# Two logarithms per head take a sooner place in the scheduler's order: a hybrid GLA and gated DeltaNet layer on one core

## The chip, the core and the metric

The kernel runs on one core of a Trainium2 chip. A core has five engines that work side by side, each through its own queue of instructions in a fixed order: TensorE (PE, matrix products; PEld is its weight load), VectorE (DVE), ScalarE (ACT, functions such as Exp and Ln), GpSimd (POOL) and SyncE (SP, which issues most transfers). Semaphores tie the queues together. The metric is the time of one execution on the device in microseconds; three runs of the kernel before have the median 2810.88 us (2809.46 to 2811.22).

## The reference

One inference step of one layer, for a prompt of 512 frames and a sample of 64 frames, all in float32:

```python
log_a = jax.nn.log_sigmoid((a_lr @ gla_wg + gla_bg).astype(f32)) / GLA_GATE_NORM
o_a, s_gla = blocked_recurrence(gla_step, st_gla, (q * dk**-0.5, k, v, log_a), block)     # 4 heads
o_a = from_heads(o_a, gla_norm) * silu(a_r)
qkv = silu(causal_dwconv(concat([b_q, b_k, b_v]), st_conv, gdn_conv_w))
o_b, s_gdn = blocked_recurrence(gdn_step, st_gdn, (l2norm(q), l2norm(k), v, g, beta), block)  # 8 heads
o_b = from_heads(o_b, gdn_norm) * silu(b_g)
x = x + g1 * (concat([o_a, o_b]) @ w_out)
x = x + g2 * conv_ffn(rmsnorm(x, norm2) * (1 + sc2) + sh2, ...)
y = rmsnorm(x, final_norm)
```

Before it stand an adaLN modulation (`silu(c) @ w_ada`) and the input projection `h @ w_in`. `gla_step` sums the gate `log_a` along the frames of a block and uses the exponentials of differences of these sums as decays. The change touches `log_sigmoid` alone.

## The kernel before, in words

Every float32 product is made of three matmuls with a high and a low part (`mm6`): a weight tile is loaded (`raw`), ScalarE rounds it to the high part (`wh`), VectorE subtracts to get the low part (`wl`); `split` does this with three buffers for each part. A projection tile of 128 columns (`in_tile`, `gemm`) takes 16 k-tiles of six matmuls each, and ends in one of two PSUM tiles `g`, from which ScalarE evicts it.

The kernel goes through a head (norm, modulation, first projections), the mixing phase (all other projections of `w_in`, with the recurrences in between), the first half of `w_out`, its second half, and the FFN with a last norm. In the mixing phase `tick` is called after each k-tile. It advances the recurrences, which are Python generators: jobs (`gdn`, `gla`, one step per tick in turn) and tasks (`gdn_conv`, `gla_gate`, every one at each tick). A planner keeps a rough clock for each engine (`charge`, called by `_Timed`), and a generator goes on only when its clock says that its results are there. This planner fixes the order in which instructions are traced.

A scheduler then sets the order on each engine from what is ready, by rank. An instruction's rank is its place in the traced order. Within `tc.high_priority(offset=80)` an instruction ranks 80 places sooner. Jobs go through `self.jv` and `self.ja`, which wrap each call so (`_Sooner`, `JOB_AHEAD = 80`, L2180 in the profile); weight conversions rank 80 sooner too (`AHEAD`). Tasks use `self.tv` and `self.ta`, which are timed in the same way but keep their place (L2204). The table loads that ScalarE needs when it changes from one set of functions to another are put in after this order is set.

`gla_gate` makes the gate of one GLA head, for the prompt (128x512, tile `m`) and the sample (128x64, tile `sq`) together. With z the projected gate it computes min(z, 0) - ln(1 + exp(-|z|)): matmuls with `wg`, an addition of the bias on VectorE, then on ScalarE two Abs, two Exp and two Ln, traced in this order in one step of the generator, then on VectorE a subtraction and the running sums (`tensor_tensor_scan`). The prompt's sums are used by the head's `gla` job; the sample's are written to memory (`put_s`, `sd_ag`) and read back by the last job, `gla_samples`, which starts with head 3. The four gates are spawned by `gla_heads`, one per head, each behind the head's `aq` and `ak` tiles. Before them, for the preceding head, stand the `ar` tiles, evicted by ScalarE with Silu into `gt` (three buffers, freed when the job has multiplied by the gate) and `ts`.

In the profile the prompt's logarithm reads `m<-m,consts` and the sample's `sq<-sq,consts`, since their bias is a constant one; Abs and Exp read `m<-m` and `sq<-sq`. All calls through a wrapper carry the wrapper's line.

Of the kernel before, what the change touches and what calls it, by code (L numbers as in the profile page):

```python
# [11 lines left out]
AF = mybir.ActivationFunctionType  # L12
# [91 lines left out]
class Kern:  # L104
# [1251 lines left out]
    def gla_gate(self, h, g, done):  # L1356

        V, A, T = self.tv, self.ta, self.jt
        y, gss, ys = self.m(), self.half()[:, :TS], self.half()[:, :TS]
        one = self.c["ones"]  # L1360
        parts = ((g, y, 0, TP, P), (gss, ys, TP, TS, TS))
        pss = [self.bank() for _ in parts]
        for ps, (z, t, c0, n, seg) in zip(pss, parts):
            T.matmul(ps[:, :n], self.wg[:, h * P:(h + 1) * P], self.na[:, c0:c0 + n], start=True, stop=True)
        for ps, (z, t, c0, n, seg) in zip(pss, parts):
            V.tensor_scalar_add(z, ps[:, :n], self.vec("gla_bg", h))
        yield from self.until()
        for z, t, c0, n, seg in parts:
            A.activation(t, z, AF.Abs)
        for z, t, c0, n, seg in parts:  # L1370
            A.activation(t, t, AF.Exp, scale=-1.0)
        for z, t, c0, n, seg in parts:
            A.activation(t, t, AF.Ln, bias=one[:, 0:1])
        self.slower("A", 2.6)
        yield from self.until()
        for z, t, c0, n, seg in parts:
            V.scalar_tensor_tensor(t, z, 0.0, t, op0=ALU.min, op1=ALU.subtract)
            scan = lambda out, b: V.tensor_tensor_scan(out, one[:, :seg], t[:, b:b + seg], 0.0, op0=ALU.mult, op1=ALU.add)
            if n == TS:
                self.put_s("ag", h, lambda out: scan(out, 0))  # L1380
            else:
                for b in range(0, n, seg):
                    scan(g[:, b:b + seg], b)
        done(self.chain + HOP_US)
# [913 lines left out]
```

## Time and profile before

| | |
|---|---|
| median of three runs | 2810.88 us (2809.46 to 2811.22) |
| profiled execution, time | 2805.69 us |
| profiled execution, span | 2804.0 us |
| TensorE busy | 2743.4 us (98%) |
| VectorE busy | 2284.9 us (81%) |
| ScalarE busy | 1314.5 us (47%) |
| GpSimd busy | 462.0 us (16%) |
| chain that ended last | PE 82%, DVE 9%, issue 3%, ACT 2%, DMA 2% |

A row of the order in time gives the start in microseconds from the start of the span, the duration, the engine, the line, the operation, the tile written and the tiles read (`out<-in`), the shapes and a count when several rows are merged; in brackets how long the engine stood idle before it and what ended that. A row of a window gives, for a stretch of time, the busy time of each engine with its count of instructions, the granted clock of TensorE (PEclk, 1.00 is full speed), the share of the DMA engines and their rate. `ACT_TABLE_LOAD` is ScalarE's change to another set of functions; it carries the line of the activation that needs it.

### The profile page before, as it was taken

The numbers are of one execution on the slowest core, as the hardware profiler recorded it, in microseconds if no ns is written. First come the engines' busy times: TensorE is split into PE (matmuls) and PEld (weight loads), VectorE is DVE, ScalarE is ACT, GpSimd is POOL, SyncE is SP. The second block draws the span as 40 slices with busy tenths as digits, with TensorE's granted clock in tenths as the row PEclk, the third lists the DMA queues.
The fourth block names the chain that finished last, engine by engine and source line by source line (L and its number), as shares of the span: only waits on it lengthen the run. The fifth ranks groups of instructions, "written<-read, shape, count | busy, mean of one in ns | idle before, by whom it ended". The sixth has DMA issues, their size and how long they took to land.

```text
span 2804.0 us, 52855 instructions
## 1 busy us (share of the span) xinstructions
PE 2743.4 (98%) x20612; PEld 2662.9 (95%) x20612; DVE 2284.9 (81%) x3721; ACT 1314.5 (47%) x2314; POOL 462.0 (16%) x437
## 2 busy tenths in 40 slices
PE   7999999999999999999999999999999999999998
PEld 4799999999999999999999999999999999999987
DVE  4578787787877887678999999999999976888886
ACT  4255555464544442355454544444454544333453
POOL 0001000010000000000333333333333300000240
PEclk9999999999999999999999999999999999999999
DMA  9965455554654657633555555464645594673751
GB/s 317 325 198 157 137 142 142 144 156 133 181 147 117 178 166 212 196 100 113 155 163 158 172 156 179 141 187 141 191 148 181 159 298 153 184 237 100 220 170 68
DMA packets 646366, 478.15 MB, mean 171 GB/s; under 512 B 65609, under 2 KB 572740, under 8 KB 646116
## 3 DMA queue, kind: packets, MB, share of 16 engines
q1 hardware_dynamic: 633012, 461.30, 55.1%
q10 hardware_dynamic: 13104, 13.47, 1.6%
q8 instruction: 162, 2.65, 0.4%
q14 instruction: 88, 0.72, 0.1%
HBM read 397.73 MB, written 76.96 MB: 169 GB/s over the span
## 4 chain that ended last, share of the span: by engine, by line
PE 82%; DVE 9%; issue 3%; ACT 2%; DMA 2%; POOL 1%; SPq 0%; ACTq 0%; DVEq 0%; POOLq 0%
PE g L647 17%; PE bank L1728 14%; PE bank L1727 14%; PE bank L1729 14%; PE g L649 8%; PE bank L2220 4%; PE g L1727 2%; PE g L1729 2%; PE g L1728 2%; DVE acc L2204 2%; PE bank L2216 1%; PE bank L869 1%; DVE wl L2204 1%; DVE wl L1632 1%; DVE m L2180 1%
## 5 line engine op out<-in xcount | busy, mean ns | idle before, releaser
L1728 PE MATMUL bank<-slot,wh 128*128 128x290 f32 (+1 forms) x3024 | 901.7, 298 | 0.0
L1727 PE MATMUL bank<-slot,wh 128*128 128x290 f32 (+1 forms) x3024 | 897.8, 297 | 1.3 <-ACT sqa L1599 1.0
L1729 PE MATMUL bank<-slot,wl 128*128 128x290 f32 (+1 forms) x3024 | 894.3, 296 | 0.4 <-DVE wl L1632 0.2
L1729 PEld LDWEIGHTS bank<-slot,wl 128*128 128x128 f32 x3024 | 574.7, 190 | 1.2 <-DVE wl L1632 1.2
L1727 PEld LDWEIGHTS bank<-slot,wh 128*128 128x128 f32 x3024 | 569.8, 188 | 5.4 <-issue 3.6
L1728 PEld LDWEIGHTS bank<-slot,wh 128*128 128x128 f32 x3024 | 571.7, 189 | 0.1
L647 PE MATMUL g<-hh,wh 128*128 128x288 f32 x2048 | 473.1, 311 | 1.9 <-ACT ts L2204 1.7
L1630 ACT ACTIVATE wh<-raw 128x1024 fp32r<-128x1024 f32 (+1 forms) x304 | 280.5, 923 | 360.8 <-PE bank L1728 260.5
L649 PE MATMUL g<-hh,wl 128*128 128x288 f32 x2048 | 442.2, 297 | 1.7 <-DVE wl L1027 1.7
L647 PE MATMUL g<-hl,wh 128*128 128x288 f32 x2048 | 442.5, 297 | 0.0
L1632 DVE TENSOR_TENSOR wl<-raw,wh 128x1024 fp32r<-128x1024 f32 (+1 forms) x304 | 371.2, 1221 | 73.1 <-ACT wh L1630 69.6
L647 PEld LDWEIGHTS g<-hh,wh 128*128 128x128 f32 x2048 | 325.3, 190 | 22.6 <-issue 15.1
L1630 ACT ACTIVATE wh<-s 128x1024 fp32r<-128x1024 f32 (+1 forms) x228 | 210.7, 926 | 283.7 <-DVE s L1643 103.4
L649 PEld LDWEIGHTS g<-hh,wl 128*128 128x128 f32 x2048 | 330.9, 189 | 5.1 <-issue 3.1
L647 PEld LDWEIGHTS g<-hl,wh 128*128 128x128 f32 x2048 | 330.6, 189 | 3.2 <-issue 2.3
L1632 DVE TENSOR_TENSOR wl<-s,wh 128x1024 fp32r<-128x1024 f32 (+1 forms) x228 | 250.5, 1100 | 14.6 <-ACT wh L1630 13.5
L2204 ACT ACTIVATE wh<-raw 128x1024 fp32r<-128x1024 f32 x135 | 142.8, 1058 | 202.9 <-PE g L647 198.1
L2204 DVE SCALAR_TENSOR_TENSOR acc<-aw,ct,acc 128x512 f32<-128x512 f32 x284 | 201.6, 746 | 3.9 <-DMA aw<-in_w_ada_dram 3.8
L2204 DVE TENSOR_TENSOR wl<-raw,wh 128x1024 fp32r<-128x1024 f32 x135 | 165.5, 1227 | 47.7 <-ACT wh L2204 45.3
L1851 POOL TENSOR_TENSOR j<-j,j 128x288 f32<-128x288 f32 (+1 forms) x120 | 186.2, 1558 | 83.7 <-ACT j L1855 82.1
L1727 PE MATMUL g<-slot,wh 128*128 128x288 f32 x560 | 167.1, 299 | 3.8 <-DVE slot L1923 2.3
L1728 PE MATMUL g<-slot,wh 128*128 128x288 f32 x560 | 165.4, 296 | 0.0
(341 smaller groups left out, 4062.6 us busy)
## 6 DMA issues: line engine op xcount, KB each, us to landing
raw<-in_w_up_dram SPq DMA_DIRECT2D x176, 512.0 KB
raw<-in_w_in_dram SPq DMA_DIRECT2D x100, 512.0 KB
raw<-in_w_down_dram SPq DMA_DIRECT2D x128, 320.0 KB
aw<-in_w_ada_dram SPq DMA_DIRECT2D x79, 512.0 KB
slot<-cd SPq DMA_DIRECT2D x140, 288.0 KB
cd<-j SPq DMA_DIRECT2D x120, 288.0 KB
xr<-in_w_ada_dram SPq DMA_DIRECT2D x49, 512.0 KB
hraw<-in_w_ada_dram SPq DMA_DIRECT2D x40, 512.0 KB
```

What stands on the lines that cost most here:

```text
L647: T.matmul(ps[:, h if bank is None else bank, :n], wh, x[:, h, :n], start=f, stop=False)
L649: T.matmul(ps[:, h if bank is None else bank, :n], wl, ah[:, h, :n], start=False, stop=stop)
L869: T.matmul(ps[32 * k:32 * k + 32, :w], cs[:, k0 + k], got[n][k // per][:, k % per], start=(k0 == 0), stop=(k0 == KD - 4))
L1630: self.nc.scalar.activation(hi, src, AF.Copy)
L1632: self.nc.vector.tensor_tensor(lo, src, hi.bitcast(F32), op=ALU.subtract)
L1727: T.matmul(ps, wh[:, j], hi, start=(c < 3 and j == 0), stop=False, skip_group_check=True)
L1728: T.matmul(ps, wh[:, j], lo, start=False, stop=False, skip_group_check=True)
L1729: T.matmul(ps, wl[:, j], hi, start=False, stop=(j == n - 1), skip_group_check=True)
L1851: minus = lambda out, a, b: G.tensor_tensor(out, a, b, op=ALU.subtract)
L2180: return f(*a, **kw)
L2204: return f(*a, **kw)
L2220: return self.engine.matmul(out, *a, **kw)
```

## The change

The two Ln of a gate are issued through `self.ja` in place of `self.ta`. Both wrappers charge the planner in the same way, so the traced order stays; the Ln rank 80 places sooner, as the steps of a job do. The Abs and Exp before them, and the VectorE steps behind them, stay as they were.

```diff
         for z, t, c0, n, seg in parts:
             A.activation(t, t, AF.Exp, scale=-1.0)
         for z, t, c0, n, seg in parts:
-            A.activation(t, t, AF.Ln, bias=one[:, 0:1])
+            self.ja.activation(t, t, AF.Ln, bias=one[:, 0:1])
         self.slower("A", 2.6)
         yield from self.until()
```

## The prediction

> **What bounds the kernel now.** I read the page first (who is busy), then the windows around the four gates, then the order of work on ScalarE and TensorE inside them.
>
> ```profile
> span 2804.0 us, 52855 instructions
> PE 2743.4 (98%) x20612; PEld 2662.9 (95%) x20612; DVE 2284.9 (81%) x3721; ACT 1314.5 (47%) x2314; POOL 462.0 (16%) x437
> ```
>
> TensorE is busy for 98% of the span and ScalarE for 47%. Work put on or taken off ScalarE counts only where TensorE waits for it. The four gates run near 690, 764, 862 and 972 us; the windows of three of them say whether TensorE waits there:
>
> ```profile
> core 0: us, PE busy (x) PEld busy (x) DVE busy (x) ACT busy (x) POOL busy (x), PEclk, DMA share, GB/s
> 686.00:712.00 26.00, 25.53 (x197) 24.01 (x196) 23.14 (x45) 15.63 (x34) 1.37 (x1) 1.00 0.55 154
> 855.00:875.00 20.00, 15.78 (x95) 14.52 (x95) 12.68 (x29) 13.05 (x21) 0.28 (x1) 0.83 0.47 148
> 964.00:992.00 28.00, 26.83 (x203) 25.29 (x203) 21.63 (x49) 15.95 (x29) 0.75 (x1) 1.00 0.60 172
> ```
>
> Around head 0 TensorE is idle for 26.00 - 25.53 = 0.47 us, around head 3 for 1.17 us; around head 2 for 4.22 us, and the granted clock there is 0.83. Head 2 is the only gate with much to win. ScalarE there, in order of time (start, duration, instruction):
>
> ```profile
> 861.99 0.63 ACT L2180 ACTIVATE m<-m 128x512 f32<-128x512 f32 x1 [0.41 <-DVE m L2180]
> 862.63 1.28 ACT L2204 ACT_TABLE_LOAD   x1
> 863.93 0.72 ACT L2204 ACTIVATE m<-m,consts 128x512 f32<-128x512 f32 x1
> 864.67 1.28 ACT L2204 ACT_TABLE_LOAD   x1
> 865.96 0.60 ACT L2204 ACTIVATE gt<-g 128x512 f32<-128x512 f32 x1
> 866.46 0.33 ACT L2204 ACTIVATE ts<-g 128x64 f32<-128x64 f32 x2
> ...
> 867.55 1.28 ACT L2204 ACT_TABLE_LOAD   x1 [0.76 <-ACT ts L2204]
> 868.85 0.35 ACT L2204 ACTIVATE sq<-sq,consts 128x64 f32<-128x64 f32 x1
> ```
>
> The activations that read `consts` are the two logarithms (their bias is the constant one). Here they are apart: between them stand a Silu eviction (`gt`, `ts`) and two table loads. And this is what TensorE does:
>
> ```profile
> 863.97 1.08 PE L2220 MATMUL bank<-qc,m 128*128 128x64 f32 x8 [2.21 <-DVE m L2180]
> 866.73 0.85 PE L647 MATMUL g<-hh,wh 128*128 128x288 f32 x2 [1.68 <-ACT ts L2204]
> 867.37 0.68 PE L647 MATMUL g<-hl,wh 128*128 128x288 f32 x2
> ...
> 872.60 0.43 PE L647 MATMUL g<-hh,wh 128*128 128x288 f32 x2
> 872.87 0.43 PE L647 MATMUL g<-hl,wh 128*128 128x288 f32 x2
> ```
>
> It waits 2.21 us for a GLA step, and then 1.68 us until the Silu eviction frees a PSUM tile. Afterwards it runs slowly: twelve pairs of matmuls take 872.60 - 866.73 = 5.87 us, where the pair at 872.60 takes 0.27, so twelve would take 3.24. The slow stretch loses 2.63 us; the whole stall is worth 4.22 + 2.63 = 6.9 us.
>
> **The change, part by part.** It removes and adds no arithmetic: eight activations (two per head) keep operands, durations (0.72 and 0.35 above) and ScalarE as their engine. They issue no DMA. The planner is charged the same, because `ja` and `ta` are both timed under "A", so every step is traced at the same tick as before. What changes is one rank: both logarithms stand 80 places sooner in the order of choice, and the two Abs and two Exp before them in the same gate do not. That gap decides what follows.
>
> How the order works can be read on VectorE near head 1, where job steps (L2180, sooner) and gate steps (L2204, later) compete:
>
> ```profile
> 770.84 0.21 DVE L2204 SCALAR_TENSOR_TENSOR sq<-sq,sq 128x64 f32<-128x64 f32 x1
> 770.98 0.18 DVE L2180 TENSOR_TENSOR m<-m 32x36 f32<-32x36 f32 x1
> 771.08 0.41 DVE L2204 TENSOR_TENSOR_SCAN m<-consts,m 128x128 f32<-128x128 f32 x1
> ```
>
> The job's chain (the inverse, rows of 0.18 us, each needing the one before) is not issued in one piece, although it ranks ahead of the gate's scans: around its step stand a gate instruction before (0.21) and one after (0.41), and so it goes on. I read that as a rule: a step that needs the instruction just issued is not ready yet, so one other ready instruction goes first; at the choice after that, the sooner rank wins. Now the same rule on ScalarE at head 1:
>
> ```profile
> 765.59 0.63 ACT L2204 ACTIVATE m<-m 128x512 f32<-128x512 f32 x1
> 766.13 0.61 ACT L2180 ACTIVATE m<-m 128x512 f32<-128x512 f32 x1
> 766.65 1.26 ACT L2180 ACTIVATE m<-m,s 128x128 f32<-128x128 f32 x4
> 767.82 0.24 ACT L2204 ACTIVATE sq<-sq 128x64 f32<-128x64 f32 x1
> 768.08 1.28 ACT L2204 ACT_TABLE_LOAD   x1
> 769.37 0.73 ACT L2204 ACTIVATE m<-m,consts 128x512 f32<-128x512 f32 x1
> 770.00 0.33 ACT L2204 ACTIVATE sq<-sq,consts 128x64 f32<-128x64 f32 x1
> 770.35 1.28 ACT L2180 ACT_TABLE_LOAD   x1
> ```
>
> The gate's prompt Exp (765.59) is followed by five job activations, and only then by its sample Exp (767.82): job steps already push the sample Exp back. With the change the prompt logarithm has a job's rank and the sample Exp still has not. After one job activation (766.13) the prompt Exp is through, the prompt logarithm is ready, and it goes ahead of the sample Exp. The order becomes Exp 512, Ln 512, Exp 64, Ln 64. Each change of function costs a load: 770.35 shows one between a logarithm and the next Exp. So head 1 gets two loads more, 2 x 1.28 = 2.57 us of ScalarE. In heads 0 and 3 one activation also stands between the prompt Exp and the sample Exp (first row from head 0, the others from head 3):
>
> ```profile
> 692.45 0.26 ACT L2204 ACTIVATE sq<-sq 128x64 f32<-128x64 f32 x1 [0.21 <-PE bank L2220]
> ...
> 972.80 0.63 ACT L2204 ACTIVATE m<-m 128x512 f32<-128x512 f32 x1
> 973.34 0.67 ACT L2180 ACTIVATE m<-bank,cols 128x512 f32<-128x512 f32 x1
> 973.91 0.24 ACT L2204 ACTIVATE sq<-sq 128x64 f32<-128x64 f32 x1
> ...
> 984.01 0.21 ACT L2180 ACTIVATE s<-qkv 128x4 f32<-128x4 f32 x1 [5.32 <-DMA qkv<-sd_ag]
> ```
>
> I expect the same there: 3 x 2.57 = 7.7 us more of ScalarE, with the prompt logarithm a little earlier and the sample logarithm 2.57 us later. The Trainium skill, ScalarE: Activation LUTs, section Table sets, says that one set holds both ln and exp, so that ln followed by exp needs a single load. By it the extra loads would fall away, and the outcome would be that of rival C below. The trace disagrees: the load at 770.35 stands right behind a logarithm and before an Exp.
>
> *Heads 0 and 1, on the path: 0 us.* What is queued behind the two loads on ScalarE are weight conversions and job evictions; VectorE's lower halves of the weights wait for the former, TensorE's job steps for the latter. Weights have three buffers, and ScalarE is idle for 26.00 - 15.63 = 10.4 us of head 0's window, so 2.57 us fit. If that cover is gone, each head costs up to 2.57 us. No gain is possible beyond the 0.47 us idle there.
>
> *Head 2, on the path: +0.3 us, between -3.7 and +1.2.* Prompt and sample Exp already stand side by side here, so the alternation above does not arise. Whether the logarithms come together depends on the Silu eviction `gt`. It was traced one projection tile earlier, 16 x 6 = 96 matmuls, more than the 80 places that the logarithms gain, so it still outranks the sample logarithm once it is ready. Low end: the eviction goes ahead of the job's Exp at 861.99 and TensorE resumes 0.63 + 0.41 = 1.04 us sooner, and the slow stretch (2.63) does not come: -3.7. High end: both logarithms go ahead of that Exp, which then needs a load of its own (1.28) before the eviction, plus 0.33 for the second logarithm, less the 0.41 us idle: +1.2. I take +0.3, the second logarithm alone slipping in ahead of the eviction, since that is nearest to the rows.
>
> *Head 3, on the path: +0.7 us, between -1.2 and +5.2.* The sample logarithm feeds a scan whose result goes to memory (`sd_ag`) and back; ScalarE waits 5.32 us for it at 984.01, in order, and TensorE behind it:
>
> ```profile
> 986.31 0.66 PE L2216 MATMUL bank<-consts,qkv 128*128 128x128 f32 x4 [1.17 <-ACT qkv L2204]
> ```
>
> If the order behind it stays, the data come 2.57 us later and TensorE's wait grows to 1.17 + 2.57 = 3.74 us; should that bring a slow stretch as at head 2, 2.63 more: +5.2. If the scheduler, which sees the later data, puts the evictions ahead of the waiting activation, the 1.17 us go. I take the middle of -1.17 and +2.57. The Trainium skill, TensorE: Matmul & The Clock Gate, section What's actually happening, has the clock fall to half after about 3.4 us without work. That agrees with the 0.83 at head 2; by it a wait of 3.74 us would be just long enough, and the sum would be nearer its high end.
>
> Later stages keep their order: the work after the last gate is traced as before. Sum: 0 + 0 + 0.3 + 0.7 = +1.0 us. The profiled execution took 2805.69 us in all (span 2804.0), 5.2 us below the median of the runs shown, 2810.88; on its own time the sum gives 2806.7, on the median 2811.9.
>
> **The rivals.**
>
> *A, slower: the extra loads reach TensorE.* For it: at head 3 a ScalarE result is already what TensorE waits for, and the change delays that result. Against it: in head 0's window TensorE has 0.47 us of idle time, so there the loads had slack. It decides where an activation that TensorE needs has less than 2.57 us to spare. Head 3 with its slow stretch (5.2) and one other head (2.57): 2810.88 + 7.8 = 2818.7.
>
> *B, faster: head 2's stall goes.* For it: 6.9 us hang on one eviction that ScalarE issued behind a logarithm and two loads. If another order of choice brings `gt` forward or other work into the gap, up to all of it is won: 2804.0. Against it: the eviction's own rank does not change, and the logarithms move ahead of it rather than behind.
>
> *C, the change does what it says.* The pairs stand together in all heads, head 2 loses one table load, nothing else moves. Then TensorE resumes at head 2 between 0.33 later and 1.04 sooner: 2809.8 to 2811.2. Against it: the unmoved sample Exps.
>
> **How the numbers follow.** Of this kernel, 0.2% (5.6 us) is about what a measurement can tell from no change. Forecast (loads added, hidden) 0.42 and C 0.12 lie within it; A 0.28 lies above; B 0.18 below. So faster 0.18, same 0.54, slower 0.28. The range runs from just below B to above A, 2803.5 to 2820: below it lies a stall that goes together with head 3's wait, above it the loads of all heads on the path (2810.88 + 5.2 + 3 x 2.57 = 2823.8 with head 2's end). The likeliest case alone: 2807 to 2816.
>
> **What would show it.** In the changed profile the logarithms carry L2180 instead of L2204. Right if, in heads 0, 1 and 3, the order on ScalarE reads Exp 128x512, load, Ln 128x512, load, Exp 128x64, load, Ln 128x64, and there are about six more table loads. Wrong if the pairs stay together there. At head 2, the idle time of TensorE in 855 to 875 (4.22 us) and the granted clock (0.83) say between forecast and B; at head 3, the wait before the transposes of `qkv` (1.17 us) says between forecast and A. The prediction fails if a new wait of several microseconds with a lowered clock shows up near any gate, or the one at head 2 vanishes.

## The result and the profile after

The changed kernel takes 2821.76 us (median of four runs, 2819.66 to 2823.46); the kernel before, run beside it, 2810.17 us. The ratio is 1.0049 with a 95% interval of 1.0037 to 1.0061: slower, by 11.6 us in the medians. The forecast was 2811.9 us, at most 2820. The profiled execution after took 2823.46 us. The head of its page:

```profile
span 2821.7 us, 52863 instructions
PE 2754.4 (98%) x20612; PEld 2673.1 (95%) x20612; DVE 2285.1 (81%) x3721; ACT 1322.4 (47%) x2320; POOL 460.8 (16%) x437
```

ScalarE has six instructions more (2320 against 2314) and 7.9 us more of busy time, of which six table loads of 1.28 us make 7.7. TensorE executes the same 20612 matmuls, but is busy 11 us longer: some of them ran slowly. Where the time came in can be read from the first Abs of each gate, which the change does not touch. ScalarE of the kernel before, one row per head (start, duration):

```profile
689.67 0.63 ACT L2204 ACTIVATE m<-m 128x512 f32<-128x512 f32 x1 [1.19 <-DVE m L2204]
...
763.50 0.63 ACT L2204 ACTIVATE m<-m 128x512 f32<-128x512 f32 x1 [1.02 <-DVE m L2204]
...
860.13 0.63 ACT L2204 ACTIVATE m<-m 128x512 f32<-128x512 f32 x1
...
970.72 0.63 ACT L2204 ACTIVATE m<-m 128x512 f32<-128x512 f32 x1 [0.16 <-DVE m L2204]
```

The same four rows of ScalarE in the changed kernel:

```profile
693.33 0.63 ACT L2204 ACTIVATE m<-m 128x512 f32<-128x512 f32 x1 [1.20 <-DVE m L2204]
...
769.62 0.63 ACT L2204 ACTIVATE m<-m 128x512 f32<-128x512 f32 x1 [1.03 <-DVE m L2204]
...
872.54 0.63 ACT L2204 ACTIVATE m<-m 128x512 f32<-128x512 f32 x1
...
983.09 0.63 ACT L2204 ACTIVATE m<-m 128x512 f32<-128x512 f32 x1 [0.16 <-DVE m L2204]
```

The distances are 3.66, 6.12, 12.41 and 12.37 us, and 17.7 us at the end of the span. So 3.66 us are lost ahead of any changed instruction, where both programs are the same; that is how two executions differ. Most of it is the clock: between 30 and 45 us and between 640 and 665 us the granted clock is 0.89 and 0.86 in the changed kernel's execution and 1.00 and 0.93 in the other, which is some 1.7 us of lost time each (an estimate: 0.11 x 15 and 0.07 x 25). Head 0 adds 2.46 us, head 1 6.29, head 2 nothing (-0.04), head 3 and what follows 5.33. The windows of the changed kernel behind the gates (columns as in the prediction) say in what form:

```profile
686.00:712.00 26.00, 23.05 (x176) 21.52 (x175) 18.46 (x43) 16.82 (x32) 1.37 (x1) 1.00 0.42 116
800.00:830.00 30.00, 27.88 (x188) 26.97 (x192) 14.21 (x29) 9.82 (x20) 0.00 (x0) 0.83 0.27 78
866.00:886.00 20.00, 15.75 (x94) 14.60 (x93) 13.48 (x32) 12.93 (x21) 1.13 (x1) 0.83 0.52 167
990.00:1020.00 30.00, 26.47 (x189) 25.66 (x188) 20.95 (x57) 12.90 (x25) 0.00 (x0) 0.89 0.28 81
```

At head 0 TensorE is idle for 26.00 - 23.05 = 2.95 us in place of 0.47, at full clock. Behind heads 1 and 3 it is idle for some 2 and 3.5 us, and the granted clock is down to 0.83 and 0.89. Head 2 has 4.25 us of idle time and a clock of 0.83, where it had 4.22 us and 0.83.

**Head 0, followed from ScalarE to TensorE.** ScalarE of the changed kernel, in order of time:

```profile
695.27 0.63 ACT L2204 ACTIVATE m<-m 128x512 f32<-128x512 f32 x1
...
696.38 1.28 ACT L2180 ACT_TABLE_LOAD   x1
697.68 0.72 ACT L2180 ACTIVATE m<-m,consts 128x512 f32<-128x512 f32 x1
...
698.58 1.28 ACT L2204 ACT_TABLE_LOAD   x1
699.88 0.26 ACT L2204 ACTIVATE sq<-sq 128x64 f32<-128x64 f32 x1
...
700.42 1.28 ACT L2180 ACT_TABLE_LOAD   x1
701.72 0.35 ACT L2180 ACTIVATE sq<-sq,consts 128x64 f32<-128x64 f32 x1
```

The pair that was to come together has come apart: Exp, load, Ln for the prompt, then load, Exp, load, Ln for the sample. VectorE of the kernel before and TensorE behind it:

```profile
695.96 0.22 DVE L2204 SCALAR_TENSOR_TENSOR sq<-sq,sq 128x64 f32<-128x64 f32 x1
...
704.44 0.42 DVE L2180 TENSOR_TENSOR m<-bank,consts 128x256 f32<-128x256 f32 x1
...
705.00 1.07 PE L2220 MATMUL bank<-m,m 128*128 128x64 f32 x8 [0.47 <-DVE m L2180]
```

And the same three in the changed kernel:

```profile
702.10 0.23 DVE L2204 SCALAR_TENSOR_TENSOR sq<-sq,sq 128x64 f32<-128x64 f32 x1 [2.98 <-ACT sq L2180]
...
710.60 0.41 DVE L2180 TENSOR_TENSOR m<-bank,consts 128x256 f32<-128x256 f32 x1
...
711.15 1.08 PE L2220 MATMUL bank<-m,m 128*128 128x64 f32 x8 [2.95 <-DVE m L2180]
```

VectorE stands 2.98 us for the sample's logarithm. Between that subtraction and the step that TensorE needs, VectorE works without a gap in both kernels (704.44 - 695.96 = 8.48 us, 710.60 - 702.10 = 8.50 us). So the delay passes through whole, and TensorE's 0.47 us become 2.95.

**Heads 1 to 3.** At head 1 the same thing happens on VectorE as at head 0. The steps of the job's inverse (rows of 32x50 and the like) are queued behind the sample's subtraction. One of them in the kernel before:

```profile
773.00 0.18 DVE L2180 TENSOR_TENSOR m<-m 32x50 f32<-32x50 f32 x1
```

The same step in the changed kernel, and the subtraction ahead of it:

```profile
779.87 0.22 DVE L2204 SCALAR_TENSOR_TENSOR sq<-sq,sq 128x64 f32<-128x64 f32 x1 [1.69 <-ACT sq L2180]
...
780.33 0.18 DVE L2180 TENSOR_TENSOR m<-m 32x50 f32<-32x50 f32 x1
```

VectorE stands 1.69 us for the sample's logarithm. The step of the inverse comes 7.33 us later than before, of which 6.12 were lost ahead of head 1: 1.21 us. When the inverse is written to memory (`d<-m`, at 786.31 before and 793.98 after) it is 1.55 us late; in between VectorE also waits 0.23 us for a copy that stands behind the loads on ScalarE (`qkv`, at 782.91). Its way back from memory (`cm<-d`) ends later, VectorE waits for it, and TensorE for VectorE. The matmul in question in the kernel before:

```profile
794.50 1.07 PE L2220 MATMUL bank<-m,m 128*128 128x64 f32 x8 [0.71 <-DVE m L2204]
```

VectorE and TensorE of the changed kernel at the same place:

```profile
800.68 1.29 DVE L2204 TENSOR_TENSOR m<-cm,consts 128x512 f32<-128x512 f32 x2 [2.04 <-DMA cm<-d]
...
802.12 1.85 PE L2220 MATMUL bank<-m,m 128*128 128x64 f32 x8 [2.21 <-DVE m L2204]
...
808.48 0.68 PE L647 MATMUL g<-hl,wh 128*128 128x288 f32 x2
...
812.79 0.43 PE L647 MATMUL g<-hl,wh 128*128 128x288 f32 x2
```

The wait grows by 2.21 - 0.71 = 1.50 us. From 802.12 to about 812 us a pair of matmuls takes 0.68 us instead of 0.43; that slow stretch is the rest of head 1's 6.29 us, 4.8 us. At head 2, where the Exps stood together before, ScalarE of the changed kernel has this order:

```profile
875.29 0.72 ACT L2180 ACTIVATE m<-m,consts 128x512 f32<-128x512 f32 x1
876.03 1.28 ACT L2204 ACT_TABLE_LOAD   x1
877.33 0.60 ACT L2204 ACTIVATE gt<-g 128x512 f32<-128x512 f32 x1
...
879.35 0.35 ACT L2180 ACTIVATE sq<-sq,consts 128x64 f32<-128x64 f32 x1
```

TensorE of the changed kernel waits for the eviction:

```profile
878.09 0.85 PE L647 MATMUL g<-hh,wh 128*128 128x288 f32 x2 [3.91 <-ACT ts L2204]
```

The Silu eviction `gt` still goes between the two logarithms. TensorE's waits of 2.21 and 1.68 us, 3.89 together, have become one of 3.91. At head 3 ScalarE waits for the sample's sums from memory as before, but that wait ends later, and TensorE waits behind it (ScalarE and TensorE of the changed kernel):

```profile
998.74 0.21 ACT L2180 ACTIVATE s<-qkv 128x4 f32<-128x4 f32 x1 [4.83 <-DMA qkv<-sd_ag]
...
1001.05 1.12 PE L2216 MATMUL bank<-consts,qkv 128*128 128x128 f32 x4 [3.53 <-ACT qkv L2204]
```

The wait is 3.53 us (before: 1.17), and pairs of 0.68 us follow. Here too VectorE stands for the sample's logarithm (2.54 us, at 991.69), so the transfer of the sample's sums (`sd_ag`) starts at 993.41 in place of 978.55, 2.49 us more than the 12.37 lost before.

### The profile page after: what moved, and what is told of

Same layout as the page of the kernel before. It is cut to its first block, busy times and chain, and to the rows that moved or that the text cites. A ratio compares the mean times of both kernels' runs of the same rounds, so it can differ in the third digit from the quotient of the medians.

```text
span 2821.7 us, 52863 instructions
## 1 busy us (share of the span) xinstructions
PE 2754.4 (98%) x20612; PEld 2673.1 (95%) x20612; DVE 2285.1 (81%) x3721; ACT 1322.4 (47%) x2320; POOL 460.8 (16%) x437
## 4 chain that ended last, share of the span: by engine, by line
PE 82%; DVE 8%; issue 3%; ACT 2%; DMA 2%; POOL 1%; SPq 0%; ACTq 0%; DVEq 0%; POOLq 0%
PE g L647 17%; PE bank L1728 14%; PE bank L1727 14%; PE bank L1729 14%; PE g L649 8%; PE bank L2220 4%; PE g L1727 2%; DVE acc L2204 2%; PE g L1729 2%; PE g L1728 2%; PE bank L2216 1%; PE bank L869 1%; DVE wl L1632 1%; DVE wl L2204 1%; DVE m L2180 1%
```

## The experiments

All times are medians, with the ratio to the kernel before in the same session and its interval. Two theories stood first. L: the six extra loads, torn from the pairs, make the loss. R: the sooner rank makes it, by moving other work.

**1. The loads without the rank.** Exp and Ln are issued in one loop, part by part, at the rank of before.

```diff
         for z, t, c0, n, seg in parts:
             A.activation(t, t, AF.Exp, scale=-1.0)
-        for z, t, c0, n, seg in parts:
             A.activation(t, t, AF.Ln, bias=one[:, 0:1])
```

> Edit: the ranks of before; only the order in which the gate's four activations are traced changes (Exp 512, Ln 512, Exp 64, Ln 64), so heads 0, 1 and 3 get two table loads more each, TensorE's order stays that of before, and head 2 stays as before. Theory L (the loads themselves delay ScalarE's queue, and TensorE waits in an order that does not move): about the whole loss of the change, 2819 to 2823 us, with new waits of some 2 us near 705, 800 and 985 us. Rival R (the new ranks cost: what is reordered around head 2, not the loads): no change, within 2 us of before.

2822.28 us, ratio 1.0054 (1.0039 to 1.0069): the whole loss, without any change of rank. Windows of this kernel at head 0, behind head 1 and behind head 3:

```profile
686.00:712.00 26.00, 22.77 (x162) 21.23 (x161) 20.55 (x41) 16.65 (x31) 1.38 (x1) 0.93 0.45 124
800.00:830.00 30.00, 28.24 (x195) 26.94 (x196) 14.70 (x30) 9.83 (x21) 0.00 (x0) 0.83 0.25 75
...
990.00:1020.00 30.00, 26.09 (x188) 25.28 (x187) 22.25 (x60) 12.60 (x25) 0.00 (x0) 0.89 0.26 75
```

The idle time stands at the same three places as in the change, and the clock behind heads 1 and 3 is down as there; at head 0 it is down too in this execution (0.93, in the change 1.00). L holds: the loads alone make the loss.

**2. The rank without the loads.** The logarithms get the job's rank, but may only be issued behind the last Exp.

```diff
-        for z, t, c0, n, seg in parts:
-            A.activation(t, t, AF.Ln, bias=one[:, 0:1])
+        with self.tc.issue_after(self.nc.cur_bb.bb.instructions[-1]):
+            [self.ja.activation(t, t, AF.Ln, bias=one[:, 0:1]) for z, t, c0, n, seg in parts]
```

> Edit: the ranks of the change, but both logarithms are queued behind the second Exp, so heads 0, 1 and 3 have the same order and the same three loads as before, and only head 2 is reordered as in the change. L: within 2 us of before. R: 8 to 12 us slower, as the change.

2807.84 us, ratio 1.0000 (0.9991 to 1.0010). Heads 0, 1 and 3 then run as before; only head 2 has the order of the change, and that order is worth nothing. R falls.

**3. The pairs together in all four heads.** As 2, with a rank 400 places sooner, so that in head 2 both logarithms go ahead of the eviction; ScalarE has one load fewer than before.

```diff
-        for z, t, c0, n, seg in parts:
-            A.activation(t, t, AF.Ln, bias=one[:, 0:1])
+        with self.tc.issue_after(self.nc.cur_bb.bb.instructions[-1]), self.tc.high_priority(offset=400):
+            [self.ta.activation(t, t, AF.Ln, bias=one[:, 0:1]) for z, t, c0, n, seg in parts]
```

> Edit: as pairs, with a rank of 400 places sooner for both logarithms, so that they stand together in head 2 too, ahead of the Silu eviction, with one table load less in all than before. L: at most 2 us from before, since head 2's eviction comes only some tenths of a us later and the load that goes stood behind it. R: 8 to 12 us slower.

2806.66 us, ratio 0.9995 (0.9986 to 1.0005): what the change set out to do, reached, cannot be told from no change. TensorE waits 4.2 us for the eviction in head 2.

**4. The change with fewer loads.** The sample's Exp becomes an Abs, for which the trace has no load; this kernel leaves the sample's exponential out, so its gate for the sample is not the reference's.

```diff
-            A.activation(t, t, AF.Exp, scale=-1.0)
+            A.activation(t, t, AF.Exp if n == TP else AF.Abs, scale=-1.0)
         for z, t, c0, n, seg in parts:
-            A.activation(t, t, AF.Ln, bias=one[:, 0:1])
+            self.ja.activation(t, t, AF.Ln, bias=one[:, 0:1])
```

> Edit: the change, with the sample's Exp replaced by a second Abs, which needs no table load; the sample's gate is therefore not computed as in the reference. The order stays that of the change; heads 0 and 3 have no extra loads, head 1 keeps its two, since a job's Exp stands between its logarithms. L: about 4 to 5 us slower than before, all of it behind head 1. R: 8 to 12 us slower.

2809.68 us, ratio 1.0008 (0.9999 to 1.0018). Heads 0 and 3 lose their extra loads here, and with them their waits and slow pairs; head 1 keeps two. The loss is 1.6 us by the medians (before: 2808.05) and 2.2 by the ratio, less than L's 4 to 5, and the interval holds no change too. What is missing in the profiled execution is the slow stretch. TensorE of this run waits behind head 1 as in the change:

```profile
797.87 1.08 PE L2220 MATMUL bank<-m,m 128*128 128x64 f32 x8 [2.42 <-DVE m L2204]
```

The window around it has a clock of 1.00, where the change had 0.83 behind head 1:

```profile
795.00:825.00 30.00, 27.58 (x223) 25.55 (x222) 17.76 (x37) 12.20 (x26) 0.00 (x0) 1.00 0.39 109
```

**5 to 7. One head at a time.** The change in head 0, in head 1 or in head 3 alone.

```diff
-            A.activation(t, t, AF.Ln, bias=one[:, 0:1])
+            (self.ja if h == 0 else A).activation(t, t, AF.Ln, bias=one[:, 0:1])
```

> Edit: the new rank in head 0 alone (two table loads more there). L: 2.5 us slower than before, TensorE's wait near 705 us grows from 0.5 to 3 us, nothing after it changes. Rival W (a loss comes only where a wait brings a slow stretch of TensorE's clock, a bare wait is made up later): no change.

> Edit: the new rank in head 1 alone (two table loads more). L: TensorE's wait near 795 us grows by 1.5 us, 1.5 us slower, and 4 to 5 us slower if the clock falls behind it as in the changed kernel. W: 0 without the slow stretch, 3 with it.

> Edit: the new rank in head 3 alone (two table loads more). L: TensorE's wait for the eviction of qkv near 986 us grows from 1.2 to 3.5 us and a slow stretch of 2.6 us follows: 5 us slower. W: 2.6 us slower.

Head 0: 2810.57 us, ratio 1.0011 (1.0002 to 1.0021). Head 1: 2811.63, 1.0012 (1.0002 to 1.0021). Head 3: 2812.25, 1.0012 (1.0003 to 1.0021). By the ratios each head alone costs about 0.12%, some 3.3 us; the three make 0.35%, the change 0.49%. By the medians (before: 2807.18) they cost 3.4, 4.5 and 5.1 us, 12.9 together, against 11.6 for the change. With intervals of 0.1% on each, the sum of the three cannot be told from the change, and how much of each cost is chance in the slow stretches stays open. Theory W, by which a bare wait is made up later, falls by head 0 of the change: there the wait stayed without a slow stretch, and 2.46 us were lost. TensorE in the run of head 0 alone:

```profile
705.22 1.08 PE L2220 MATMUL bank<-m,m 128*128 128x64 f32 x8 [2.96 <-DVE m L2180]
...
707.16 0.68 PE L647 MATMUL g<-hh,wh 128*128 128x288 f32 x2
```

The wait is that of the change (2.96 against 2.95), but here slow pairs follow it for 3 us, where the change had none. In the run of head 3 alone the window 975 to 1010 shows both parts of its cost, 35.00 - 31.08 = 3.92 us of idle time and a clock of 0.90:

```profile
975.00:1010.00 35.00, 31.08 (x223) 30.27 (x222) 23.33 (x63) 17.29 (x30) 0.00 (x0) 0.90 0.34 99
```

**8. The dose doubled in head 0.** Head 0 alone, with the ranks of before and the four steps in a fixed order: the sample's gate in two halves, each with its Exp and its Ln, so that four loads are added; the other heads as before.

```diff
...
+        steps = [(AF.Exp, y), (AF.Exp, ys), (AF.Ln, y), (AF.Ln, ys)]
+        steps = steps if h else [(f, t) for t in (y, ys[:, :32], ys[:, 32:]) for f in (AF.Exp, AF.Ln)]
+        for k, (f, t) in enumerate(steps):
...
```

> Edit: the ranks of before; in head 0 alone the sample's Exp and Ln are done in two halves one after the other, four table loads more than before in place of the change's two (and two short activations and a weight conversion ahead of the job's eviction). L: twice the delay of head 0, TensorE's wait near 705 us some 6 to 7 us long, with a slow stretch behind it: 7 to 10 us slower. A rival by which the first loads only used up slack that a longer wait also meets once (a wait for something else that ends at the same time): 2.5 us, as with two.

2813.87 us, ratio 1.0023 (1.0014 to 1.0032), 6.5 us, twice the loss of two loads. L had expected 7 to 10 us and a wait of 6 to 7 us; TensorE's wait there is 4.48 us, with slow pairs behind it. The dose was not doubled cleanly: in this run VectorE does the prompt's sums and one accumulation ahead of the sample's subtraction, where it waits 3.98 us.

**9. The way by which the loads reach TensorE.** The change in head 0 alone, with VectorE's subtraction for the sample issued behind the prompt's sums and one accumulation.

```diff
-            A.activation(t, t, AF.Ln, bias=one[:, 0:1])
+            (self.ja if h == 0 else A).activation(t, t, AF.Ln, bias=one[:, 0:1])
...
-            V.scalar_tensor_tensor(t, z, 0.0, t, op0=ALU.min, op1=ALU.subtract)
...
+            with self.tc.issue_after(self.nc.cur_bb.bb.instructions[-1]) if h == 0 and n == TS else nullcontext(): V.scalar_tensor_tensor(t, z, 0.0, t, op0=ALU.min, op1=ALU.subtract)
```

> The change in head 0 alone (measured before: +2.5 to +4 us, TensorE's wait behind the sample's logarithm 2.96 us, VectorE's 2.97 us), with one thing added: in head 0 VectorE's subtraction that reads the sample's logarithm is issued behind the prompt's four sums and one accumulation (4 x 0.34 + 0.75 = 2.1 us of other work) in place of ahead of them. ScalarE still has the two extra loads. Theory V (the loads reach TensorE through VectorE, which stands in order behind the late logarithm): VectorE's wait falls to about 0.9 us, TensorE's wait near 705 us from 2.96 to about 1 us, window 690 to 716 back to about 25 us of busy TensorE, no slow stretch; the time within 0 to +1.5 us of the kernel before. Rival S (the loads reach TensorE through ScalarE's own queue, conversions and evictions behind them): moving VectorE's subtraction changes nothing, wait about 3 us and +2.5 to +4 us again.

2807.50 us, ratio 1.0007 (0.9996 to 1.0017). The time alone does not decide, since its interval holds the 1.0011 of run 5; the trace does. VectorE of this run:

```profile
700.91 0.22 DVE L2204 SCALAR_TENSOR_TENSOR sq<-sq,sq 128x64 f32<-128x64 f32 x1 [1.03 <-ACT sq L2180]
```

TensorE of this run, at the matmul that waited 2.96 us in run 5:

```profile
708.15 1.08 PE L2220 MATMUL bank<-m,m 128*128 128x64 f32 x8 [1.15 <-DVE m L2180]
```

VectorE waits 1.03 us instead of 2.98, TensorE 1.15 instead of 2.96, and no pair of 0.68 us follows. The loads are all still there. So in head 0 the cost goes through VectorE's order, as theory V said. (A weight conversion also moved ahead of one load on ScalarE; in run 5 VectorE did not wait for that conversion, so it is not the cause.)

**10 and 11. A fourth buffer for `gt`.** Head 2's stall hangs on the eviction into `gt`. Run 3 with a fourth buffer, whose space is taken from `m`, or from `qkv`.

```diff
-    BUFS = {"m": 17, "qkv": 8, "gt": 3}
+    BUFS = {"m": 16, "qkv": 8, "gt": 4}
```

> The version with the pairs together in all four heads (ratio 0.9995 before), and a fourth buffer for the Silu eviction gt, its space taken from m (17 to 16 buffers). In the order on ScalarE the eviction of head 2 then stands ahead of the gate instead of behind it, for one more table load. Theory E (head 2's stall hangs on this eviction): TensorE's wait for ts near 866 us (4.2 us there, 3.9 with the change) goes, the clock in 855 to 875 rises from 0.83 to near 1, and the time is 4 to 7 us below the kernel before, ratio about 0.998. Rival Q (TensorE meets another wait at the same place, for a GLA step or for one of the m buffers that are now fewer): the idle time of that window stays at 3 to 5 us and the ratio between 0.9995 and 1.002.

> As the run before it, but the space for the fourth gt buffer is taken from qkv (8 to 7 buffers). Theory E: the same gain, ratio about 0.998, since it is the eviction that counts. Rival Q: qkv tiles come free later, conv tasks and evictions into qkv wait, TensorE waits for ACT qkv longer than the 1.2 us at head 3; ratio 0.9995 to 1.003. If m16 and q7 differ by more than 0.1%, it is the buffer taken away that decides.

2798.51 us, ratio 0.9970 (0.9960 to 0.9981), and 2799.57 us, ratio 0.9973 (0.9964 to 0.9982). The first is the fastest version, 8.4 us below the kernel before. Its window at head 2, where the kernel before had 15.78 us and a clock of 0.83:

```profile
855.00:875.00 20.00, 20.00 (x146) 19.12 (x146) 14.43 (x31) 9.93 (x18) 1.13 (x1) 1.00 0.57 158
```

TensorE has no gap left there. The eviction goes ahead of the gate, as theory E said, and which buffer is taken away does not matter. With `m` at 16 the program has the same order on every engine whether the logarithms are edited or not, so the gain is the buffer's alone; the fourth buffer without that edit was not timed on its own.

**12. The change on top of that.** The fourth buffer (`m` at 16) and the change; all four pairs are torn, eight loads more, TensorE's order the same as in run 10.

> The change on top of the faster version of the kernel before (fourth gt buffer, m with 16; 2798.5 us, ratio 0.997). TensorE's order is the same as there; ScalarE has eight table loads more, since the two logarithms are now torn apart in all four heads, head 2 too. Theory L (each torn pair makes two loads, and they reach an in-order TensorE that has no slack near the gates): three heads cost what they cost in the change, 0.35 to 0.49 percent, and head 2, no longer hidden by the stall behind its eviction, up to 2.6 us more: ratio to the kernel before 1.001 to 1.003, with waits of TensorE of 2 to 4 us at heads 0, 1 and 3. Rival K (the loss of the change came from its meeting with head 2's stall or from another run state, not from the loads): ratio below 0.999.

2812.65 us, ratio 1.0019 (1.0010 to 1.0027): 0.49 points above run 10, as much as the change cost before; the two runs are compared through the kernel before, each in its own session. TensorE's waits in this run between 150 and 1140 us (sum, times, longest):

```profile
PE bank L2220 <- DVE m L2204: 8.2, 3, 3.7
PE bank L2216 <- ACT qkv L2204: 5.1, 2, 3.6
PE bank L2220 <- DVE m L2180: 3.0, 1, 3.0
```

The window of head 2 in this run, which holds the torn pair (logarithms at 873.23 and 877.35):

```profile
870.00:900.00 30.00, 30.00 (x240) 29.52 (x239) 21.84 (x47) 16.83 (x27) 0.00 (x0) 1.00 0.33 95
```

In run 10 the same three sums are 6.5, 2.7 and 0.5 us. Heads 0, 1 and 3 wait as in the change; head 2 has two extra loads and no idle time at all. The 2.6 us that theory L allowed for head 2 did not come.

## Why the prediction was wrong

- *The order.* Right. A step that depends on the instruction just issued lets one other go first, so the sooner logarithm tears its own pair apart in heads 0, 1 and 3: two loads each, 6 x 1.28 = 7.7 us forecast, 7.9 us measured on ScalarE.
- *"Heads 0 and 1, on the path: 0 us"* is the step that failed. They cost 2.46 and 6.29 us in the profiled execution, and about 0.12% each alone. The cover was computed on the wrong engine: ScalarE's idle 10.4 us and three weight buffers hide a late conversion (VectorE waits for none behind the loads of head 0). They do not hide a late operand of VectorE, which takes its queue in order: everything behind the sample's subtraction waited with it, up to the step that TensorE needs. Run 9 shows this for head 0; for heads 1 and 3, where VectorE stood 1.69 and 2.54 us, it is read from the trace, and no run moved the subtraction there. The prediction followed what is queued behind the loads on ScalarE, and not what is queued on VectorE behind the reader of the late logarithm. That TensorE was idle for only 0.47 us was read as slack; it said how late the operand already was. The bound of 2.57 us per head, should the cover fail, held for head 0 in the profiled execution; head 1 went beyond it by the slow stretch, which the bound left out, and so did head 0 alone in run 5 (3.4 us by the medians).
- *Head 2, +0.3 us.* Right within that term: nothing. The eviction kept its place between the logarithms by its rank, as argued; the second logarithm, for which the 0.3 us stood, did not slip in ahead of it. The low end, the eviction first and the stall gone, did not come; runs 10 and 11 show that it takes a buffer, not a rank.
- *Head 3, +0.7 us.* The mechanism was right and the size was not. The term was taken as the middle between the ends; the high end, 5.2 us (a wait of 3.74 us and a slow stretch), is what happened: 3.53 us of wait and 5.33 us in all. The scheduler did not put the evictions ahead of the waiting activation. The 0.83 at head 2 does not bear out what the prediction cites for the clock, as it says it does: the longest wait there was 2.21 us, and work stood between it and the next of 1.68.
- *The rule on sets of functions.* By the Trainium skill, ScalarE: Activation LUTs, section Table sets, ln and then exp need one load. The changed kernel disagrees as the kernel before did: between the sample's Exp at 699.88 and the logarithm ahead of it stands a load at 698.58.
- *Rivals.* A is what happened (2818.7 forecast, 2821.76 measured): head 3 with its slow stretch and another head. It took all three heads. B needs the fourth buffer; C, the pairs together, was made in run 3 and is worth nothing that can be measured.

The sum by rows, 3.66 + 2.46 + 6.29 - 0.04 + 5.33 = 17.7 us, is that of one execution. Without the part ahead of the gates it is 14.0 us, against 11.6 in the medians; slow stretches that come in some executions only can make such a difference, but no run settles it.

## What to carry to other kernels

Before a delay is called hidden, follow it along every engine in order: from the late result to the engine that reads it, to what stands behind that reader in its queue, and only then ask whether the next engine has time. A rank moves one step, not the group that makes it cheap: if two steps share a table load, tie the pair together, or the scheduler will fill the gap between them with the thing that tears them apart. And a stall that looks like a matter of rank can be one of buffers; one more buffer won 0.3% where no order of the logarithms won anything.

## What the runs showed of the hardware

Short waits of TensorE can bring a slow stretch, but not each time. After 2.95 us at head 0 the changed kernel ran on at full clock; after 2.96 us at the same matmul, run 5 had 3 us of slow pairs. Behind head 1, waits of 2.21 us (the change), 2.19 us (run 6) and 2.42 us (run 4) were followed by half clock for 10.24 us, for 3.41 us, and not at all. All stretches of half clock near the gates, in every trace of this case, last 3.41 us or two or three times that. TensorE of run 6:

```profile
799.74 1.08 PE L2220 MATMUL bank<-m,m 128*128 128x64 f32 x8 [2.19 <-DVE m L2204]
...
804.53 0.68 PE L649 MATMUL g<-hh,wl 128*128 128x288 f32 x2
```

The Trainium skill, TensorE: Matmul & The Clock Gate, section What's actually happening, puts the fall of the clock after an idle window of about 3.4 us, in a window that runs freely. The lengths of the stretches agree with such a window, and that the effect changes from run to run agrees with its running freely; that 2.2 us of waiting were enough does not agree with a window wholly without work. So the price of a wait of 2 to 3 us here was its length, and at times half of 3.4 to 10.2 us more, some 2 to 5 us.
